# Attention scores of four tiles issued in one run, with the pooling matmuls and the values placed around them

## The chip, the core and the metric

The kernel runs on one core of a Trainium2 chip. The metric is device time in microseconds (us), the median of three runs of the whole program. The engines are named as the profile does: PE is TensorE's matmul pipe and PEld its weight loads, DVE is VectorE, ACT is ScalarE, POOL is GpSimd, SP is SyncE, which here only issues DMA transfers. Each engine works through its own instructions in order; engines wait for each other by semaphores.

## The reference, cut to what matters

The reference is one decoder block on x of 1024 positions by 1024 channels: a half-step feed-forward network, a mixer, a second half-step network, a final norm. The mixer projects the normed rows to q, k, v (12 heads of 64), to a pooling input and to two gates, and merges two branches:

```python
y_attn = dilated_mixture_attention(q, k, v) @ w_branch_attn[l]
y_pool = multiscale_pool(pz, pool_w[l], pool_scale[l]) @ w_branch_pool[l]
merged = gates[:, :, 0] * y_attn + gates[:, :, 1] * y_pool
h = h + merged @ w_out[l]
```

The attention has three groups of four heads, with windows and dilations (128, 1), (512, 4) and (2048, 16). In a group the positions with equal residue form a subsequence; each block of 128 queries of it sees its own block of keys and, where there is one, the block before, masked to a trailing window. Per query there are a maximum m of the scores, p = exp(s - m), its sum l, and the output p @ v / l. The three groups of a head slot are then weighted by their softmax denominators and added.

## The kernel before, in words

Everything is float32. A product is made of three matmuls on split operands (`three`: high x high, high x low, low x high), where high is a rounded copy and low the rest. Before the attention stage comes the projection of the mixer (line 332), behind it the branch product and merge (lines 1756 to 1776) and the second network. The change lies in the attention stage alone, between these two.

**Tiles and pairs.** The work is 48 tiles in order: head pair 0 with groups 0, 1, 2, then head pair 1 with groups 1, 2, 0, eight tiles of 128 queries in each. A tile treats two heads (a = 0, 1). It is *narrow* (one block of 128 keys) or *wide* (two blocks, 256 keys): group 0 has one narrow tile and seven wide ones, group 1 alternates, group 2 has narrow ones only. Two tiles form a pair q = 0 to 23, and the loop over q is a software pipeline written out by hand under a manual schedule: what is written first is issued first on its engine. Pairs 0 to 3 are group 0, 4 to 7 group 1, 8 to 11 group 2, 12 to 15 group 1, 16 to 19 group 2, 20 to 23 group 0.

**What is done for a pair**, each by a function with the name given:

- `scores` (L1553, tile `s`): per tile three terms for each of two heads, 12 matmuls of 64 rows, into two PSUM banks of the tag `mm`, one for each head.
- `masked` (L1571, tile `e`): on DVE, four custom operations, each adds mask and scale and takes the maximum of one head of one tile, with a short read of the accumulator (`stats`) behind each. Below these are called the maxima. They free the score banks.
- `exponents` (L1580): on ACT, four exponentials with their sums.
- `trans_p` (L1600, tile `tp`): 4, 6 or 8 transposes on PE into one or two banks of the tag `acc`.
- `split_p`: the high part on ACT (L1612, `ehi`) and the low part on DVE (L1615, `elo`); the low part frees the transposes' banks.
- `values` (L1633, tile `o`): 6, 9 or 12 matmuls into one bank of the tag `acc`.
- `gather` (L1651): four copies on DVE out of that bank into the rows of the group's output; below, the copies. They free the bank.

**Fills.** The pooling branch's product (`branch`, L1703, tile `yp`) is 16 chains of 12 matmuls. It is a generator, and each `next(fill)` issues four of them, called a fill; three fills end a chain, which holds one bank of the tag `acc`. `end_branches` then multiplies the chain's bank by a gate on DVE (L1717, tile `gb`: the gate product), which frees it. Every second chain ends a branch block: its rows are stored (L1726) and the weights and the gate of a later block are loaded (`load_branch`, L1241 and L1242).

**Banks.** `mm` and `acc` have four banks each. A new tile takes the bank that was released longest ago in program order, and its first writer waits on the semaphore of the last reader. From step 18 to 21 the tag `mm` is used by `factor_rows` too (L1534, tile `fa`: four transposes a time), whose banks are read by the products on DVE (L1670, tile `o`) of the first head pair's combination.

**One step q before.** PE: scores of q; transposes of q-1; two fills (one where q % 4 is 3); the factor rows, where there are any; values of q-2. DVE: copies of q-3; maxima of q; low part of q-1; products with the factor rows; gate products of the chains that ended. ACT: high part of q-1; parts of the next ring of q and k operands (L1213, with the low part on POOL, L1214); exponents of q. `house` and `load_ring` issue the small transfers: row statistics, values, the next ring (L1206). After the loop follow the transposes, values and copies that are left, the last fills and the combination of head pair 1. A reciprocal on DVE (L1514) in step 17 waits for sums on POOL (L1513).

Of the kernel before, what the change touches and what calls it, by code (L numbers as in the profile page):

```python
# [16 lines left out]
P = 128  # L17
# [8 lines left out]
HD = 64  # L26
SC = HD ** -0.5
GROUPS = 3
# [8 lines left out]
def tokens(g, i):  # L37

    if g == 0:
        return i * P, 1, (i - 1 if i > 0 else None)  # L40
    if g == 1:
        r, b = divmod(i, 2)
        return r + 4 * P * b, 4, (i - 1 if b else None)
    return i, 8, None
# [74 lines left out]
def three(hi_lo_l, hi_lo_r):  # L119

    lh, ll = hi_lo_l
    rh, rl = hi_lo_r
    return ((lh, rh), (lh, rl), (ll, rh))
# [3 lines left out]
def tile_block(  # L127
# [29 lines left out]
    ve, ac, gp, pe = nc.vector, nc.scalar, nc.gpsimd, nc.tensor  # L157
# [10 lines left out]
    def bank(tag, name):  # L168
        return psum.tile([P, HALF], F32, tag=tag, name=name)
# [1029 lines left out]
    ring = {}  # L1199
# [160 lines left out]
    with tc.manual_schedule():  # L1360
# [4 lines left out]
        for k in range(len(items) + 4):  # L1365
# [6 lines left out]
            if k < len(items):  # L1372
                q, m = items[k]
# [3 lines left out]
            if k - 1 in results:  # L1377
                q, m = items[k - 1]
# [40 lines left out]
    def open_w_o():  # L1419
        wo_pools.append(wo.enter_context(sbuf(f"wo{len(wo_pools)}", "right")))  # L1420
# [46 lines left out]
    slots = [(hp, g, i) for hp in range(HPAIRS) for g in ((0, 1, 2), (1, 2, 0))[hp] for i in range(NT)]  # L1467
    N = len(slots)
# [68 lines left out]
    def blocks(g, i):  # L1537

        return 1 if tokens(g, i)[2] is None else 2

    T = {}

    def scores(s):
        hp, g, i = slots[s]
        u = hp * GROUPS + g
        n = blocks(g, i)
        ks = slice((i + 1 - n) * P, (i + 1) * P)
        ps = [bank("mm", f"s{s}_{a}")[:, :n * P] for a in range(2)]
        (qhi, qlo, _), (khi, klo, _) = ring[u]
        for j, (l, r) in enumerate(three((qhi, qlo), (khi, klo))):  # L1550
            for a in range(2):
                rows = slice(a * HD, (a + 1) * HD)
                pe.matmul(ps[a], l[rows, i * P:(i + 1) * P], r[rows, ks], start=(j == 0), stop=(j == 2))  # L1553
        T[s] = {"s": ps}

    def masked(s):
        hp, g, i = slots[s]
        d = T[s]
        n = blocks(g, i)
        m0 = 0 if n == 2 else (128 if g < 2 else 256)  # L1560
        p = d.pop("s")
        if g == 0:
            st = stats[hp][:, 0, i, :]
        else:
            if i == 0:
                own_stats[hp, g] = att_small.tile([P, NT, 4], F32, name=f"own_stats{hp}_{g}")
            st = own_stats[hp, g][:, i, :]
        e = ep.tile([P, 4 * P], F32, tag="e", bufs=4, name=f"e{s}")
        e = e[:, :2 * n * P].rearrange("p (a c) -> p a c", a=2)
        for a in range(2):  # L1570
            ve.tensor_tensor_reduce(e[:, a, :], p[a], mask[:, m0:m0 + n * P], -SC, -NEG, OP.add, OP.min,  # L1571
                                    accum_out=st[:, a:a + 1])
        d.update(e=e, st=st)
# [11 lines left out]
    def pair(q):  # L1585

        ns = [2 * blocks(*slots[s][1:]) * P for s in (2 * q, 2 * q + 1)]
        return ((2 * q, 0, ns[0]), (2 * q + 1, ns[0], ns[1])), sum(ns)
# [16 lines left out]
    def split_p(q):  # L1605

        tiles, n = pair(q)
        hi = a2.tile([P, 2 * HALF], F32R, tag="ehi", name=f"ehi{q}")
        lo = a2.tile([P, 2 * HALF], F32R, tag="elo", name=f"elo{q}")
        todo = tp.pop(q)  # L1610
        for p, c0, w in todo:
            ac.activation(hi[:, c0:c0 + w], p, AF.Copy)  # L1612
        yield
        for p, c0, w in todo:
            ve.tensor_tensor(lo[:, c0:c0 + w], p, hi[:, c0:c0 + w].bitcast(F32), op=OP.subtract)  # L1615
        for s, c0, w in tiles:
            T[s]["pt"] = tuple(t[:, c0:c0 + w].rearrange("p (a b c) -> p a b c", a=2, c=P) for t in (hi, lo))
        yield

    def values(q):  # L1620
        both = bank("acc", f"o{q}")
        for s in (2 * q, 2 * q + 1):
            hp, g, i = slots[s]
            d = T[s]
            n = blocks(g, i)

            p = both[:, s % 2 * 2 * P:(s % 2 + 1) * 2 * P].rearrange("p (a c) -> p a c", a=2)
            pt = d.pop("pt")
            j, end = 0, 3 * n - 1
            for b in range(n):  # L1630
                c = slice((i + 1 - n + b) * P, (i + 2 - n + b) * P)
                for l, r in three(tuple(v[:, c] for v in v_of[hp * GROUPS + g]), tuple(w[:, :, b, :] for w in pt)):
                    pe.matmul(p, l, r, start=(j == 0), stop=(j == end))  # L1633
                    j += 1
            d["o"] = p
            if i == NT - 1:
                del v_of[hp * GROUPS + g]
# [3 lines left out]
    def gather(s):  # L1641

        hp, g, i = slots[s]
        p = T.pop(s)["o"]
        t0, step, _ = tokens(g, i)
        cols = slice(t0, t0 + step * (P - 1) + 1, step)
        if i == 0:
            own[hp, g] = sums_o.tile([P, S], F32, tag="o", bufs=HPAIRS * GROUPS, name=f"o{hp}_{g}")
        for a in range(2):
            r = slice(a * HD, (a + 1) * HD)  # L1650
            ve.tensor_copy(own[hp, g][r, cols], p[r, a, :])  # L1651
# [72 lines left out]
    def send():  # L1724
        while stores:
            nc.sync.dma_start(*stores.pop())  # L1726

    def branches():
        for n in range(2 * KT):
            yield from branch(n)  # L1730

    fill = branches()
# [45 lines left out]
    def advance(gen, n=1):  # L1778
        for _ in range(n):
            next(gen, None)  # L1780
# [24 lines left out]
    with tc.manual_schedule():  # L1805
        load_ring(uses[1], ring_tile)
        load_branch(1)
        factors = [make_factors(hp, eng) for hp, eng in enumerate((gp, ve))]
        combines = [[Combine(hp, half, adds, lower) for half in range(2)]
                    for hp, (adds, lower) in enumerate((((gp, gp), gp), ((gp, ve), ve)))]  # L1810
        splits = {}
        for q in range(N // 2):
            send()
            u, i = divmod(q, NT // 2)
            if 0 < u < len(uses) - 1 and i == 0:
                load_ring(uses[u + 1], ring_tile)
            scores(2 * q)
            scores(2 * q + 1)
            if q == 1:
                next(fill)  # L1820
                next(fill)
            if q > 0:
                trans_p(q - 1)
                splits[q - 1] = split_p(q - 1)
            if q > 1:
                next(fill, None)
                if q % 4 != 3:
                    next(fill, None)
            if q > 2:
                gather(2 * q - 6)  # L1830
                gather(2 * q - 5)
            masked(2 * q)
            masked(2 * q + 1)

            j = q - N // 4 - 6
            fa = [combines[0][j // 2]] * (2 - j % 2) if 0 <= j < 4 else []
            for f in fa:
                f.rows()
            if q > 1:
                values(q - 2)  # L1840
            if q > 0:
                advance(splits[q - 1], 2)
            for n in ((), (0,) if u > 0 else (), (2, 1) if u > 0 else (0, 2), (3,) if u > 0 else (1, 3))[i]:
                if u + 1 < len(uses):
                    split_ring(uses[u + 1], n)
            for f in fa:
                f.product()
            end_branches()
            exponents(2 * q)
            exponents(2 * q + 1)  # L1850
            house(2 * q)
            house(2 * q + 1)
        send()
        right_b.close()
        load_ya(3)
        load_merge(0)
        load_merge(1)
        open_w_o()
        q = N // 2
        trans_p(q - 1)  # L1860
        splits[q - 1] = split_p(q - 1)
        advance(factors[1])
        next(fill, None)
        values(q - 2)
        gather(2 * q - 6)
        gather(2 * q - 5)
        advance(splits[q - 1], 2)
        advance(factors[1], 2)
        next(fill, None)
        end_branches()  # L1870
        values(q - 1)
        for s in range(2 * q - 4, 2 * q):
            gather(s)
        for n in range(8):
            combines[1][n // 4].step()
            if n != 3:
                next(fill, None)
            end_branches()
            send()
            if n == 3:  # L1880
                load_merge(2)
        for k in (3, 4):
            load_merge(k)
# [34 lines left out]
    ops, banks = {}, {}  # L1918
# [66 lines left out]
    with tc.manual_schedule():  # L1985
# [66 lines left out]
        r = [rows_first2(t) for t in range(2)]  # L2052
# [211 lines left out]
```

## Time and profile before

| what | us |
|---|---|
| median of three runs (1908.35 to 1908.94) | 1908.75 |
| the profiled execution | 1909.05 |
| its span, first to last instruction | 1907.2 |
| PE busy / DVE busy / ACT busy / POOL busy | 1894.9 / 1337.5 / 760.0 / 731.2 |
| attention stage, first scores to first branch product | 1042.7 to 1159.8 |
| mean granted TensorE clock | 0.999 of full speed |

In the rows below, times are from the start of the span. "busy" is the union of the instructions of an engine in a stretch; PE's instructions are pipelined, so a busy PE can still start its matmuls late, and the distance between the starts of two matmuls tells more than their durations. DVE's rows overlap by up to 0.1 us at their ends as well, so its costs are taken from starts too. An idle time in brackets names what ended the wait.

### The profile page before, as it was taken

What the parts mean: (1) busy time and instruction counts of PE and PEld (TensorE: products, weight loads), DVE (VectorE), ACT (ScalarE), POOL (GpSimd) and SP (SyncE); (2) the same over time, 40 slices, a digit from 0 to 9 for tenths busy, and PEclk for the clock granted to TensorE, in tenths of its full rate; (3) what the DMA queues carried; (4) which work ended last, traced back from release to release, by engine and by line L of the source; (5) the groups of instructions that cost most, each with busy time, mean ns of one, the idle gap of its engine ahead of it and who ended that gap; (6) DMA issues with size and microseconds to landing.
All of it is one profiled execution on the core that took longest, in us unless ns stands there. A gap on an engine that the chain in (4) does not pass through costs nothing.

```text
span 1907.2 us, 24938 instructions
## 1 busy us (share of the span) xinstructions
PE 1894.9 (99%) x8946; PEld 1574.4 (83%) x8946; DVE 1337.5 (70%) x2017; ACT 760.0 (40%) x1364; POOL 731.2 (38%) x548
## 2 busy tenths in 40 slices
PE   9999999999999999999999999999999999999998
PEld 8888888888888888888888888888888888888886
DVE  7776556557776776667875896887665556577777
ACT  6323333333344443334444772353333323333344
POOL 5333333331233355444544456553333333312132
PEclk9999999999999999999999999999999999999999
DMA  4155222336466627655667977743433223454564
GB/s 189 50 193 177 83 88 105 138 110 215 148 233 219 204 92 248 220 213 196 229 231 288 305 231 262 269 149 121 164 120 124 84 88 116 149 194 138 194 219 166
DMA packets 144940, 331.98 MB, mean 174 GB/s; under 512 B 19120, under 2 KB 39856, under 8 KB 143280
## 3 DMA queue, kind: packets, MB, share of 16 engines
q1 hardware_dynamic: 137280, 308.00, 46.4%
q10 hardware_dynamic: 7536, 22.39, 3.3%
q8 instruction: 70, 1.15, 0.3%
q14 instruction: 54, 0.44, 0.1%
HBM read 229.61 MB, written 100.73 MB: 173 GB/s over the span
## 4 chain that ended last, share of the span: by engine, by line
PE 96%; DVE 1%; issue 1%; POOL 1%; ACT 1%; DMA 0%; SPq 0%; POOLq 0%; ACTq 0%; DVEq 0%
PE d_f L754 22%; PE u_mixm L332 18%; PE wo L1955 4%; PE yp L1703 2%; PE o L1633 1%; PE ya L1768 1%; PE s L1553 1%; PE u_f20b L332 1%; PE u_f11a L332 1%; PE u_f20a L332 1%; PE u_f11b L332 1%; PE u_f210b L332 1%; PE u_f210a L332 1%; PE u_f29b L332 1%; PE u_f29a L332 1%
## 5 line engine op out<-in xcount | busy, mean ns | idle before, releaser
L754 PE MATMUL d_f<-bhi_f,ahi_f 128*128 128x512 f32 x616 | 240.4, 390 | 0.0
L754 PE MATMUL d_f<-bhi_f,alo_f 128*128 128x512 f32 x616 | 239.8, 389 | 0.0
L754 PE MATMUL d_f<-blo_f,ahi_f 128*128 128x512 f32 x616 | 239.7, 389 | 0.0
L716 POOL TENSOR_TENSOR alo_f<-g_f,ahi_f 128x512 fp32r<-128x512 f32 x60 | 83.4, 1408 | 292.9 <-ACT ahi_f L712 285.7
L332 PE MATMUL u_mixm<-xhi_t_mix,wc_mixm 128*128 128x512 f32 x608 | 194.9, 391 | 0.1
L332 PE MATMUL u_mixm<-xhi_b_mix,wc_mixm 128*128 128x512 f32 x456 | 149.0, 392 | 0.0
L754 PEld LDWEIGHTS d_f<-bhi_f,alo_f 128*128 128x128 f32 x616 | 115.6, 188 | 24.2 <-DVE alo_f L716 0.3
L754 PEld LDWEIGHTS d_f<-bhi_f,ahi_f 128*128 128x128 f32 x616 | 115.6, 188 | 24.0 <-DVE xlo_b_mix L411 0.2
L754 PEld LDWEIGHTS d_f<-blo_f,ahi_f 128*128 128x128 f32 x616 | 115.6, 188 | 23.9
L332 PEld LDWEIGHTS u_mixm<-xhi_t_mix,wc_mixm 128*128 128x128 f32 x608 | 114.0, 188 | 24.3 <-POOL wc_mixm L309 0.8
L332 PE MATMUL u_mixm<-xlo_t_mix,wc_mixm 128*128 128x512 f32 x304 | 118.4, 389 | 0.0
L309 POOL TENSOR_TENSOR wc_mixm<-s_mixm,wc_mixm 128x512 fp32r<-128x512 f32 x52 | 73.5, 1415 | 101.7 <-ACT wc_mixm L304 90.6
L332 PEld LDWEIGHTS u_mixm<-xhi_b_mix,wc_mixm 128*128 128x128 f32 x456 | 85.6, 188 | 17.8 <-issue 0.3
L304 ACT ACTIVATE wc_mixm<-s_mixm 128x512 fp32r<-128x512 f32 x76 | 47.0, 628 | 117.3 <-DVE s_mixm L364 56.9
L332 PE MATMUL u_mixm<-xlo_b_mix,wc_mixm 128*128 128x512 f32 x228 | 88.8, 389 | 0.0
L712 ACT ACTIVATE ahi_f<-g_f 128x1024 fp32r<-128x1024 f32 x84 | 81.8, 974 | 2.3 <-DMA g_f<-gs_f 2.3
L309 POOL TENSOR_TENSOR wc_mixm<-raw,wc_mixm 128x512 fp32r<-128x512 f32 x40 | 61.0, 1530 | 44.1 <-ACT wc_mixm L304 37.2
L712 ACT ACTIVATE bhi_f<-s_f2w 128x512 fp32r<-128x512 f32 x55 | 32.7, 627 | 95.4 <-DVE s_f2w L732 87.8
L332 PEld LDWEIGHTS u_mixm<-xlo_t_mix,wc_mixm 128*128 128x128 f32 x304 | 57.1, 188 | 11.6
L712 ACT ACTIVATE bhi_f<-s_f1w 128x512 fp32r<-128x512 f32 x55 | 32.9, 629 | 84.0 <-DVE s_f1w L732 79.1
L716 DVE TENSOR_TENSOR alo_f<-g_f,ahi_f 128x1024 fp32r<-128x1024 f32 (+1 forms) x48 | 57.6, 1200 | 7.7 <-ACT ahi_f L712 7.7
L1955 PE MATMUL wo<-w_o,o_hi 128*128 128x512 f32 x224 | 60.2, 390 | 0.0
(1321 smaller groups left out, 5079.8 us busy)
## 6 DMA issues: line engine op xcount, KB each, us to landing
g_f<-gs_f SPq DMA_DIRECT2D x70, 512.0 KB
gs_f<-y_f SPq DMA_DIRECT2D x88, 256.0 KB
raw<-in_w2a_dram SPq DMA_DIRECT2D x35, 512.0 KB
raw<-in_w2b_dram SPq DMA_DIRECT2D x35, 512.0 KB
gs_f<-gb_f SPq DMA_DIRECT2D x46, 256.0 KB
raw<-in_w1a_dram SPq DMA_DIRECT2D x22, 512.0 KB
raw<-in_w3a_dram SPq DMA_DIRECT2D x22, 512.0 KB
raw<-in_w1b_dram SPq DMA_DIRECT2D x22, 512.0 KB
```

The lines of the kernel that those rows point to most:

```text
L304: ac.activation(w[:, 0], src, AF.Copy)
L309: eng.tensor_tensor(w[:, 1], src, w[:, 0].bitcast(F32), op=OP.subtract)
L332: pe.matmul(p, a, b, start=(start and i == 0), stop=(i == 11), skip_group_check=not start)
L712: ac.activation(hi[:, c], src, AF.Copy)
L716: eng.tensor_tensor(lo[:, d], src[:, o], hi[:, d].bitcast(F32), op=OP.subtract)
L754: pe.matmul(self.banks[m][t], l, r, start=(first and q == 0), stop=(last and q == 2))
L1553: pe.matmul(ps[a], l[rows, i * P:(i + 1) * P], r[rows, ks], start=(j == 0), stop=(j == 2))
L1633: pe.matmul(p, l, r, start=(j == 0), stop=(j == end))
L1703: pe.matmul(p, a, b, start=(j == 0), stop=(j == 11))
L1768: pe.matmul(p, a, b, start=(j == 0), stop=(j == 5))
L1955: pe.matmul(banks[m][t], l, r, start=(st == 0 and n == 0), stop=(st == 1 and n == 5))
```

## The change

Three things are moved; the arithmetic, the number of instructions and the transfers stay.

1. `scores` takes a pair, and both tiles of the pair share their two banks: tile 2q in the columns 0 to 255, tile 2q+1 in 256 to 511. Two pairs then fill the four `mm` banks, and a step with even q (a *long* step) issues the scores of q and of q+1 together. A step with odd q (a *short* step) issues none.
2. Values stand directly behind the transposes in a long step, ahead of its fills. A long step has two fills, a short one has one, and where q % 4 is 2 (but for q = 22) the long step has a third, which stands ahead of the factor rows and of the gate products.
3. In a long step DVE has the copies of q-3 ahead of the maxima of q, as before; in a short step the maxima come first. The factor rows stand behind the values in both.

```diff
-    def scores(s):
-        hp, g, i = slots[s]
...
-        ps = [bank("mm", f"s{s}_{a}")[:, :n * P] for a in range(2)]
+    def scores(q):
+
+        banks = [bank("mm", f"s{q}_{a}") for a in range(2)]
+        for s in (2 * q, 2 * q + 1):
+            hp, g, i = slots[s]
...
+            c0 = s % 2 * 2 * P
+            ps = [b[:, c0:c0 + n * P] for b in banks]
...
-            scores(2 * q)
-            scores(2 * q + 1)
+
+            even = q % 2 == 0
+            if even:
+                scores(q)
+                scores(q + 1)
             if q == 1:
                 next(fill)
                 next(fill)
             if q > 0:
                 trans_p(q - 1)
                 splits[q - 1] = split_p(q - 1)
+            if q > 1 and even:
+                values(q - 2)
             if q > 1:
                 next(fill, None)
-                if q % 4 != 3:
+                if even:
                     next(fill, None)
-            if q > 2:
+            if even and q > 2:
                 gather(2 * q - 6)
                 gather(2 * q - 5)
             masked(2 * q)
             masked(2 * q + 1)
+            if not even and q > 2:
+                gather(2 * q - 6)
+                gather(2 * q - 5)
 
             j = q - N // 4 - 6
             fa = [combines[0][j // 2]] * (2 - j % 2) if 0 <= j < 4 else []
-            for f in fa:
-                f.rows()
-            if q > 1:
+            if q > 1 and not even:
                 values(q - 2)
             if q > 0:
                 advance(splits[q - 1], 2)
+            if q % 4 == 2 and q < N // 2 - 2:
+                next(fill, None)
+            for f in fa:
+                f.rows()
```

The total of the fills up to the end of the loop is 40 in both; in steps 2 to 22 the new order is ahead by one fill at times (it has a third one in steps 2, 6, 10, 14 and 18, where the old order had two in every step but each fourth). The last lines of the step are as before: products with the factor rows, gate products, exponents, `house`.

More of the change, by code (lines that the diff above doesn't have):

```diff
@@ L1541, in tile_block @@
     T = {}
-    def scores(s):
-        hp, g, i = slots[s]
-        u = hp * GROUPS + g
-        n = blocks(g, i)
-        ks = slice((i + 1 - n) * P, (i + 1) * P)
-        ps = [bank("mm", f"s{s}_{a}")[:, :n * P] for a in range(2)]
[L1549 to L1554, printed above, removed]
+    def scores(q):
+        banks = [bank("mm", f"s{q}_{a}") for a in range(2)]
+        for s in (2 * q, 2 * q + 1):
+            hp, g, i = slots[s]
+            u = hp * GROUPS + g
+            n = blocks(g, i)
+            ks = slice((i + 1 - n) * P, (i + 1) * P)
+            c0 = s % 2 * 2 * P
+            ps = [b[:, c0:c0 + n * P] for b in banks]
+            (qhi, qlo, _), (khi, klo, _) = ring[u]
+            for j, (l, r) in enumerate(three((qhi, qlo), (khi, klo))):
+                for a in range(2):
+                    rows = slice(a * HD, (a + 1) * HD)
+                    pe.matmul(ps[a], l[rows, i * P:(i + 1) * P], r[rows, ks], start=(j == 0), stop=(j == 2))
+            T[s] = {"s": ps}
     def masked(s):
```

## The prediction

> **What bounds the kernel now.** I read the page first, then the granted clock and busy time by stretch, then the chain of work inside the attention stage, then single steps engine by engine.
>
> ```profile
> PE 1894.9 (99%) x8946; PEld 1574.4 (83%) x8946; DVE 1337.5 (70%) x2017; ACT 760.0 (40%) x1364; POOL 731.2 (38%) x548
> ...
> PE 96%; DVE 1%; issue 1%; POOL 1%; ACT 1%; DMA 0%; SPq 0%; POOLq 0%; ACTq 0%; DVEq 0%
> ```
>
> TensorE (PE) sets the end almost everywhere, so the change must be judged by how long PE takes for the attention stage, from 1042.4 us to the branch product at 1159.9 us. Nothing else is moved. The stage by stretches (columns: length, then busy time of PE, PEld, DVE, ACT, POOL, then clock, DMA share, GB/s):
>
> ```profile
> 1042.40:1054.20 11.80, 11.23 (x79) 8.30 (x77) 7.69 (x30) 10.05 (x29) 1.65 (x2) 1.00 1.03 395
> 1054.20:1077.50 23.30, 23.30 (x193) 20.62 (x192) 19.40 (x73) 17.63 (x59) 8.55 (x7) 1.00 0.87 302
> 1077.50:1118.90 41.40, 41.40 (x326) 35.87 (x322) 37.75 (x145) 31.48 (x111) 22.50 (x21) 1.00 0.87 270
> 1118.90:1146.40 27.50, 27.50 (x212) 23.91 (x211) 27.00 (x95) 18.46 (x63) 14.67 (x13) 1.00 0.72 222
> ```
>
> PE is full, but look at the third busy figure: VectorE (DVE) works 37.75 of 41.40 us and then 27.00 of 27.50 (98%). In steps 18 to 23 there are two bounds side by side. I write q for a step and its pair of tiles.
>
> **The gain.** Scores use 64-row matmuls; everything around them uses 128 rows. PE's rows around one set of scores:
>
> ```profile
> 1085.37 0.28 PE L1633 MATMUL o<-elo,v_in 128*128 128x256 f32 x1
> 1085.49 0.28 PE L1633 MATMUL o<-ehi,v_in 128*128 128x256 f32 x1
> 1085.70 0.33 PE L1553 MATMUL s<-qk_hi,qk_hi 64*128 64x128 f32 x2
> 1085.86 0.28 PE L1553 MATMUL s<-qk_in,qk_hi 64*128 64x128 f32 x2
> 1085.98 0.27 PE L1553 MATMUL s<-qk_hi,qk_in 64*128 64x128 f32 x2
> ...
> 1086.31 0.28 PE L1553 MATMUL s<-qk_hi,qk_in 64*128 64x128 f32 x2
> 1086.52 0.66 PE L1600 MATMUL tp<-ident,e 128*128 128x128 f32 x4
> ```
>
> Within values the next starts 0.12 later, into scores 0.21; the first scores take 0.16 instead of 0.12; out of them 0.21 instead of 0.11. That is 0.09 + 0.04 + 0.10 = 0.23, and the transposes behind scores lose a little more: eight take 1.02 there and 0.96 behind values (rows below). I take 0.3 us for one entry and exit. Steps 3, 5, ... 23 lose theirs: 11 x 0.3 = 3.3 us. At the start PE idles 11.80 - 11.23 = 0.57 us, mostly before the scores of step 1, which now find two untouched banks: another 0.6 (bounds 0 and 1.0). Largest gain 3.9 us.
>
> **What the steps become.** No matmul, copy or transfer is added. PE groups (start, time to the end of the group):
>
> ```profile
> 1118.16 0.82 PE s L1553 x12
> 1118.97 0.59 PE tp L1600 x4
> 1119.56 1.85 PE yp L1703 x8
> 1121.41 0.87 PE fa L1534 x8
> 1122.29 0.71 PE o L1633 x6
> ...
> 1131.62 1.17 PE s L1553 x12
> ...
> 1136.61 0.91 PE s L1553 x12
> ...
> 1142.36 1.02 PE tp L1600 x8
> ...
> 1144.31 1.44 PE o L1633 x12
> 1145.74 0.96 PE tp L1600 x8
> ```
>
> For narrow tiles a long step is now two scores 1.5 (0.82 + 0.82 less a switch), transposes 0.4, values 0.8, two fills 1.85 (three: 2.75): 4.5 or 5.5 us. A short step is transposes, one fill 0.95, values: 2.2 us. DVE's work stays the same in each step, and it stands in one queue. Its rows of steps 18, 7 and 21:
>
> ```profile
> 1118.75 0.25 DVE L1514 RECIPROCAL top<-top 128x16 f32<-128x16 f32 x1 [0.93 <-POOL top L1513]
> 1118.92 1.54 DVE L1651 COPY o<-o 64x128 f32<-64x128 f32 x4
> 1120.49 0.29 DVE L1571 CUSTOM_DVE_ANT_0 e<-s,mask 128x128 f32<-128x128 f32 x1
> ...
> 1121.34 0.69 DVE L1615 TENSOR_TENSOR elo<-tp,ehi 128x512 fp32r<-128x512 f32 x1
> 1121.94 1.28 DVE L1670 TENSOR_TENSOR o<-o,fa 128x512 f32<-128x512 f32 x2
> 1123.13 1.64 DVE L1651 COPY o<-o 64x128 f32<-64x128 f32 x4
> ```
>
> ```profile
> 1074.91 0.29 DVE L1571 CUSTOM_DVE_ANT_0 e<-s,mask 128x128 f32<-128x128 f32 x1
> ...
> 1076.03 1.02 DVE L1615 TENSOR_TENSOR elo<-tp,ehi 128x256 fp32r<-128x256 f32 x2
> 1076.96 0.68 DVE L1717 TENSOR_TENSOR gb<-yp,gb 128x512 f32<-128x512 f32 x1
> 1077.56 0.38 DVE L1651 COPY o<-o 64x128 f32<-64x128 f32 x1
> ```
>
> ```profile
> 1133.68 0.42 DVE L1571 CUSTOM_DVE_ANT_0 e<-s,mask 128x256 f32<-128x256 f32 x1
> ...
> 1135.07 1.02 DVE L1615 TENSOR_TENSOR elo<-tp,ehi 128x256 fp32r<-128x256 f32 x2
> ```
>
> By differences of starts: copies 1.6 (1.2 for undilated tiles, next fence), maxima 0.85 / 1.1 / 1.4 (four narrow, mixed, four wide), low part 0.6 / 0.95 / 1.2, product 0.6, gate product 0.6. So DVE needs 3 to 5 us in a short step in which PE has 2.2 to 3.4. It must have worked ahead in the long step, and there its queue stops: the gate product (and the products with fa) of a long step stand **before** the maxima of the short one and need PE's last work of the long step.
>
> PE in turn waits for DVE by the banks. In the built program values of steps 3, 5, 7, 13, 15, 21 and 23 go into the bank that the values of the step before left, and this is free only after its copies, which the short step now puts behind the maxima. Before, the copies stood first and the scores and fills covered them. That such a wait is paid in full is seen once, in the tail, where fills end early:
>
> ```profile
> 1146.38 1.19 DVE L1651 COPY o<-o 64x128 f32<-64x128 f32 x4
> ```
>
> ```profile
> 1147.00 0.63 PE L1703 MATMUL yp<-xhi_b_mix,wab 128*128 128x512 f32 x2
> 1147.71 0.36 PE L1633 MATMUL o<-ehi,v_in 128*128 128x256 f32 x1
> ```
>
> Copies end at 1147.57, values start at 1147.71: 0.1 us behind.
>
> **The walk.** Times from the start of the step named.
> Step 6 (mixed): scores 1.6, transposes 2.2, values 3.4, three fills 6.2. DVE: copies 1.2, maxima 2.4, low part 3.5, then the gate product of the branch that ends with the third fill: 6.2 to 6.85; maxima of step 7 to 8.0; copies to 9.6. PE in step 7: transposes to 6.75, fill (its bank waits for the gate product, 0.2) to 7.9, values only at 9.7. **Lost 2.0.**
> Step 12: DVE's copies end at 2.4 (it comes 0.75 late), maxima 3.5, low part 4.1, gate 4.7, maxima of 13 to 5.85, copies to 7.45. PE would have values at 6.3, gets them at 7.5: **lost 1.2.** Step 15 loses 0.2. Steps 9, 11 and 17 find their banks free. Up to step 18: start -0.6, eight switches -2.4, waits +3.4, some 0.1: step 18 starts 0.5 late.
> Step 18: PE scores 1.5, transposes 1.9, values 2.7, three fills 5.45, fa 6.3. DVE: the reciprocal waits for POOL as before, to 1.55, copies 3.15, maxima 4.0, low part 4.6, **idle to 6.0** for fa, two products 7.2, gate 7.8, maxima of 19 8.65, copies 10.3, low part 10.9, product 11.5. PE: transposes 6.7, fill 7.65, values (bank of the gate product) 8.75, fa 9.2; scores of 20 from 9.4; those of 21 need the bank of that last fa: 11.6 instead of 10.1, **lost 1.5**. The row of 1131.62 (1.17 against 0.91) is the same wait before, 0.26.
> Step 20: PE transposes 12.9, values 13.7, fills 15.55, fa 16.4. DVE copies 13.15, maxima 14.3, low part 14.9, idle to 16.0, products 17.2, gate 17.8, maxima of 21 19.2, copies 20.8. PE: transposes 17.0, fill waits for the gate to 17.9 (**0.9**), values for the copies, 18.8 to 20.9 (**2.1**), then 0.8 and fa 0.45: step 22 starts at 22.35. Before: 1136.61 - 1118.16 = 18.45. Lost 3.9 net.
> Step 22: fills end 27.9, gate 28.55, maxima 29.95, copies 31.15; values 31.25 instead of 29.75 (**1.5**), end 32.7. Before: 1145.74 - 1118.16 = 27.6. Lost 5.1 net.
> The tail has the same order, PE and DVE enter it equally late, so it hides nothing. Sum: 0.5 + 5.1 = **5.6 us later**. The profiled execution took 1909.05 (span 1907.2), 0.3 above the median 1908.75; from the median 1914.35.
>
> **Costs taken as nothing.** Activations keep their order; in a short step the transposes need exponents that have had the values and fills of the long step (2.6 us and more) as cover. SyncE's queue changes: the load of the third ring now stands behind a gate load and a store that wait for the end of branch 1.
>
> ```profile
> 1048.48 2.95 SPq L1206 DMA_DIRECT2D qk_in<-qk  x2
> ```
>
> At 395 GB/s each 0.52 MB takes 1.3 us; issued near 1059 with three in front it lands near 1064, and its first split stands behind the transposes of step 5, near 1065. If late, exponents queue behind it on ACT: 0 to 2 us.
>
> **Rivals.** (a) PE decides: if copies and gates never hold it, 1908.75 - 3.9 = 1904.9. For it: PE fills every stretch; against: the banks above. It decides if DVE's idle in long steps stays below about 0.5. (b) DVE decides and its order costs nothing: PE's gain is lost, idle DVE time is made up in the early stretch (19.40 of 23.30), so 1908.7. Against: from 1118.90 on there are 0.5 us to make up from. [...] (c) Worse: exponents or the ring's load late as well, 0.3 in each of 11 short steps: 1917.7.
>
> **How the numbers follow.** Forecast 0.55, (a) 0.10, (b) 0.22, (c) 0.13. The forecast's own range is 1912.0 to 1916.7: waits of 9.5 us (5.6 + 3.9), a quarter either way. About 0.2% (3.8 us) is what a measurement of this kernel tells from no change. Faster than that: half of (a), 0.05. Within: the rest of (a), (b) and a tenth of the forecast, 0.33. Slower: 0.62. The range 1906.0 to 1918.5 leaves out half of (a), the upper part of (c) and the forecast's ends.
>
> **What would show it.** Right: PE (or its weight loads) waiting for DVE's copies in the odd steps, 6 to 9 us in all, the largest in steps 7, 13, 21 and 23; DVE idle before gate products and products with fa; twelve score groups of 24 matmuls with one 0.2 us entry each; the stretch of steps 18 to 23 lengthened by 5. Wrong: copies that end before PE's short-step fill does, or values that start behind the fill without a gap; then DVE ran ahead and (a) or (b) holds.

## The result, and the profile after

The changed kernel takes 1916.92 us (median of six runs, 1914.16 to 1921.01) against 1908.85 us for the kernel before (six runs, 1908.35 to 1909.92): 1.0045 times as long, 95% interval 1.0035 to 1.0056. The forecast was 1914.4 with a range of 1906.0 to 1918.5. In the changed kernel the lines of the functions stand 4 lower: scores L1557, maxima L1575, transposes L1604, values L1637, copies L1655, product with fa L1674, fills L1707, gate product L1721.

The profiled execution took 1920.11 (span 1917.7). Its page, busy time and the chain:

```profile
PE 1898.2 (99%) x8946; PEld 1579.5 (82%) x8946; DVE 1338.6 (70%) x2017; ACT 760.0 (40%) x1364; POOL 730.1 (38%) x548
...
PE 94%; DVE 2%; issue 1%; POOL 1%; ACT 1%; DMA 0%; SPq 0%; POOLq 0%; ACTq 0%; DVEq 0%
```

The whole page hardly differs from before: PE still has 99%, and only its share of the chain fell from 96% to 94%. The stretches that the prediction used show more (length, busy PE, PEld, DVE, ACT, POOL, then granted clock, DMA share, GB/s):

```profile
1042.40:1054.20 11.80, 11.59 (x92) 9.31 (x91) 8.75 (x37) 10.69 (x32) 2.55 (x2) 1.00 1.04 389
1054.20:1077.50 23.30, 21.67 (x167) 19.07 (x165) 18.28 (x67) 17.18 (x56) 7.63 (x6) 0.97 0.84 300
1077.50:1118.90 41.40, 40.12 (x306) 35.07 (x305) 35.51 (x140) 28.42 (x99) 18.57 (x16) 0.93 0.80 242
1118.90:1146.40 27.50, 23.38 (x174) 19.98 (x174) 21.52 (x69) 14.69 (x52) 17.04 (x18) 0.90 0.66 203
```

PE was full in the last three of these before; now, in the same stretches of time, it lacks 1.63, 1.28 and 4.12 us, and, what the prediction has nothing of, the granted clock is below 1. What PE waited for in the stage, and what DVE waited for (us in total, times, longest):

```profile
PE o L1637 <- DVE o L1655: 5.7, 4, 1.8
PE s L1557 <- DVE o L1674: 1.3, 1, 1.3
PE yp L1707 <- DVE gb L1721: 0.9, 1, 0.9
PE o L1637 <- DVE gb L1721: 0.2, 1, 0.2
```

```profile
DVE gb L1721 <- PE yp L1707: 7.5, 6, 2.5
...
DVE o L1674 <- PE fa L1534: 3.5, 3, 1.6
```

The first group is the forecast wait: values for copies, four times (steps 7, 13, 21 and 23). The second is the other half of the circle: DVE idles for PE's last fill and last fa of a long step, and then PE waits until DVE has caught up. The chain through step 21 (start, length, what) shows it in one row after another:

```profile
1136.73 0.45 PE fa L1534 x4
1137.17 0.02 issue
1137.20 1.29 DVE o L1674 x2
1138.48 0.60 DVE gb L1721
...
1140.12 0.34 DVE e L1575
...
1141.56 0.40 DVE o L1655
1141.96 0.14 issue
1142.10 1.62 PE o L1637 x6
```

fa, two products, gate product, four maxima, four copies, and only then PE's values. For 4.9 us (1137.20 to 1142.10) the chain lies on DVE alone.

The clock's part, by stretches cut where it changes:

```profile
1076.27:1083.10 6.83, 6.83 (x45) 6.49 (x44) 3.83 (x15) 1.44 (x5) 0.00 (x0) 0.50 1.13 329
...
1141.13:1147.95 6.82, 5.85 (x37) 5.33 (x38) 5.09 (x17) 1.10 (x3) 1.77 (x2) 0.50 0.96 273
```

Twice TensorE runs at half clock for 6.83 us, each time right behind or in one of the stalls (steps 7 and 21). The six runs of the kernel fall in three groups: 1914.16 at a mean clock of 0.999; 1916.16, 1916.75 and 1917.10 at 0.997 to 0.998; 1920.11 and 1921.01 at 0.995. Only the trace of 1920.11 is kept, with its two stretches; by their mean clock the other groups fit none and one. If so, the first stretch costs 2.6 us (the middle of the second group less the first) and two cost 6.4, about 3 us each, and without any the loss is 1914.16 - 1908.85 = 5.3 us, which rests on a single run.

### The profile page after: what moved, and what is told of

Its sections match the earlier page's. It is cut to its first block, busy times and chain, and to the rows that moved or that the text cites. A ratio compares the mean times of both kernels' runs of the same rounds, so it can differ in the third digit from the quotient of the medians.

```text
span 1917.7 us, 24947 instructions
## 1 busy us (share of the span) xinstructions
PE 1898.2 (99%) x8946; PEld 1579.5 (82%) x8946; DVE 1338.6 (70%) x2017; ACT 760.0 (40%) x1364; POOL 730.1 (38%) x548
## 4 chain that ended last, share of the span: by engine, by line
PE 94%; DVE 2%; issue 1%; POOL 1%; ACT 1%; DMA 0%; SPq 0%; POOLq 0%; ACTq 0%; DVEq 0%
PE d_f L754 22%; PE u_mixm L332 18%; PE wo L1969 4%; PE yp L1707 2%; PE o L1637 1%; PE ya L1772 1%; PE u_f11a L332 1%; PE u_f20b L332 1%; PE u_f20a L332 1%; PE u_f11b L332 1%; PE u_f26a L332 1%; PE u_f15a L332 1%; PE u_f210b L332 1%; PE u_f210a L332 1%; PE u_f29b L332 1%
```

## The experiments

**Theory 1**: PE loses by waiting for DVE in the short steps, because the long step's products and gate products and then the maxima stand in DVE's one queue ahead of the copies; the stalls also bring the half clock. **Rivals**: grouping the scores is itself the loss; DVE's load decides in whatever order; the half clock has nothing to do with the stalls. The edits are shortened to what matters. Each run stands against the kernel before on the same chip; its medians were 1909.21 (the first four), 1908.66 (the next four), 1908.93 (the three after these) and 1909.00 (the last).

**Copies first again in the short steps.** The other parts of the change stay.

```
-            if even and q > 2:
+            if q > 2:
                 gather(2 * q - 6); gather(2 * q - 5)
             masked(2 * q); masked(2 * q + 1)
-            if not even and q > 2:
-                gather(2 * q - 6); gather(2 * q - 5)
```

> The changed kernel, but in the short steps the copies stand ahead of the maxima again, as before the change. Theory 1 (PE waits for DVE because the copies stand behind the maxima and the gate product in one queue; after such a stall the granted clock halves for 6.83 us): the waits of values for copies, 1.2 to 1.8 us each in steps 7, 13, 21 and 23, shrink by the 0.85 to 1.4 us of the maxima, 4.5 to 5 us in all, some of it paid again as a wait of the long steps' transposes for late exponents; no stretch at clock 0.5; 1908 to 1911. Rival (grouping the scores itself costs the time, or DVE's load does whatever its order): 1914 or more.

Measured: 1912.32 (10 runs), 3.11 above before, ratio 1.0018 (1.0008 to 1.0027); clock 0.999. PE's waits:

```profile
PE s L1557 <- DVE o L1674: 0.9, 2, 0.5
PE yp L1707 <- DVE gb L1721: 0.9, 1, 0.9
PE o L1637 <- DVE o L1655: 0.8, 2, 0.5
PE s L1557 <- DVE own_stats L1575: 0.6, 1, 0.6
PE tp L1604 <- ACT e L1584: 0.4, 1, 0.4
```

The wait for copies falls by 4.9 us (5.7 to 0.8), as theory 1 said, and the half clock is gone from the profiled run. But 1.0 us comes back behind maxima and exponents, which are now late, and the time lies 1.3 above the expected 1911: the rest of the change, with fills, values and fa in their new order, loses 3 us even with copies first. DVE has the same work as in the changed kernel here, so the order alone gave back 8.07 - 3.11 = 5.0 us, the half clock included; this refutes that DVE's load decides in whatever order.

**The third fill moved to the short step.**

```
-            if q % 4 == 2 and q < N // 2 - 2:
-                next(fill, None)
...
-                if even:
+                if even or (q % 4 == 3 and q < N // 2 - 1):
                     next(fill, None)
```

> The changed kernel, but the third fill of the steps 2, 6, 10, 14 and 18 stands in the short step behind it, behind that step's own fill and ahead of its values. Theory 1: the gate product no longer stands ahead of the short step's maxima there and PE has 0.95 us more of its own to do; the wait of step 7 (1.5 us) and the first stretch at half clock go, those of steps 21 and 23 stay, and step 21 may still halve the clock: 1909 to 1913. Rival (the place of the fills does nothing, DVE's load decides): 1914 to 1920.

Measured: 1913.96 (7 runs), 4.75 above before. Step 7's wait and its half clock are gone, but the total of the waits for copies is hardly smaller, since step 19 has a new one:

```profile
PE o L1637 <- DVE o L1655: 5.2, 4, 1.8
```

The time lies 1.0 above the upper end of what theory 1 gave and just under the rival's 1914: both ranges are missed, and the run tells little between them, except that step 21's wait stays and the clock behind it is halved for one 3.41 us stretch, in the profiled run.

**PE kept busy in the waits.**

```
+        for _ in range({4: 6, 12: 7, 13: 5}.get(n, 0)):
+            pe.matmul(p, *todo[0], start=True, stop=True)
```

> The changed kernel, with 6, 7 and 5 more matmuls of 128x512 at the start of the fills of steps 7, 21 and 23: each repeats the fill's first product, which the next one overwrites, so that PE works where it otherwise waits for the copies. That adds 18 x 0.23 = 4.1 us of work in waits of 1.5, 1.76 and 1.2 us. Theory 1: the work lies in the waits, no stretch falls to half clock, and the time is that of the changed kernel without such a stretch: 1913.5 to 1915 in every run, with a spread under 1 us, and faster than the changed kernel's median although PE does more. Rival (the half clock has another cause): the clock stays at 0.995 to 0.998 of full in the span and the time at 1916 to 1921.

Measured: 1915.48 (five runs, 1914.05 to 1916.84), 6.27 above before. The profiled run has no half clock anywhere in the stage:

```profile
1042.40:1160.00 117.60, 112.96 (x867) 97.23 (x866) 100.22 (x363) 80.84 (x264) 47.51 (x43) 1.00 0.80 258
```

PE does 4 us more, and the median lies 1.4 us under the changed kernel's, but the runs of the two overlap, so that the gain is not clear of noise. That the clock stays up in the profiled run speaks for the stalls as the cause of the half clock; but two of the five runs (1916.81 and 1916.84) still have a clock of 0.998, so "in every run" was wrong, and the median lies above the expected 1915. The waits in steps 13 and 20 were not filled. The spread, 2.8 us, is less than the changed kernel's 6.9.

**The scores grouped, and nothing else.** The loop of before, but for this:

```
-            scores(2 * q); scores(2 * q + 1)
+            if q % 2 == 0:
+                scores(q); scores(q + 1)
```

Here scores(q) writes both tiles of a pair, as in the change.

> The kernel before, with only the scores of two pairs set together in the even steps: fills two, two, two, one, copies ahead of the maxima, values behind the fills, rows of fa ahead of values, all as before. Theory 1 (grouping gains 0.3 us for each of 11 switches and 0.6 at the start, and the order of the rest makes the losses): 1905 to 1909, no wait over 1 us for copies and no half clock. Rival (an even step's long run of scores and a short step's lack of them starve DVE and PE by turns in any order): 1912 or more.

Measured: 1908.14 (10 runs), 1.07 below before, ratio 0.9995 (0.9986 to 1.0004); clock 0.999. Grouping is no loss. How much it gains is read from the starts of the scores in steps 0, 20 and 22, first of the kernel before, then of this one:

```profile
1042.67 0.33 PE L1553 MATMUL s<-qk_hi,qk_hi 64*128 64x128 f32 x2
...
1126.52 0.33 PE L1553 MATMUL s<-qk_hi,qk_hi 64*128 64x128 f32 x2
...
1136.54 0.39 PE L1553 MATMUL s<-qk_hi,qk_hi 64*128 64x256 f32 x2
```

```profile
1041.97 0.33 PE L1557 MATMUL s<-qk_hi,qk_hi 64*128 64x128 f32 x2
...
1123.85 0.32 PE L1557 MATMUL s<-qk_hi,qk_hi 64*128 64x128 f32 x1
...
1134.88 0.39 PE L1557 MATMUL s<-qk_hi,qk_hi 64*128 64x256 f32 x2
```

From the first scores to step 20: 83.85 before, 81.88 now, a gain of 1.97; to step 22: 93.87 and 92.91, a gain of 0.96. (The expectation of the next run but one speaks of 2.67 and 1.66: these still hold 0.70 by which the whole stage began earlier.) The forecast term was 3.9, of which 3.3 by step 20 (0.6 and nine switches). The starts of PE's groups between the scores of step 2 and those of step 20 show where the rest went. Scores and values together take 2.6 us less (15.80 + 20.00 before, 13.83 + 19.35 now), 0.29 for each of nine switches, so the price of an entry and exit was read rightly. Transposes take 0.8 more (11.29 and 12.07) and fills 0.3 more, and up to step 2 the gain was 0.4, not 0.6. What the transposes lose fits a wait that the grouping adds, their weight loads for exponents; of before and of this kernel:

```profile
PEld tp L1600 <- ACT e L1580: 1.3, 4, 0.5
```

```profile
PEld tp L1604 <- ACT e L1584: 3.1, 11, 0.4
```

**Half of the short steps' copies on ACT.** 
```
+            if a == 1 and s // 2 % 2 == 0 and s // 2 + 3 < N // 2:
+                ac.activation(own[hp, g][r, cols], p[r, a, :], AF.Copy)
+            else:
                 ve.tensor_copy(own[hp, g][r, cols], p[r, a, :])
```

> The changed kernel, its order untouched, but in the short steps one of the two copies of each tile is made by ACT, so DVE's queue there is two copies (0.75 us) shorter. Theory 1 (values wait in the short steps for the copies at the end of DVE's queue, and the half clock comes from these waits): the four waits of 1.2 to 1.8 us become 0.4 to 1.1 us, no stretch at half clock, 1909.5 to 1912. Rival (the place of the copies in the queue is not what holds PE, or ACT becomes the late one): 1914 or more.

Measured: 1923.93 (four runs), 15.27 above before: far outside theory 1's range, and in the rival's, which allowed for ACT becoming the late one. The first row is what ACT waited for, then the copies of step 7:

```profile
ACT o L1656 <- DVE o L1658: 25.3, 21, 3.6
```

```profile
1074.41 0.37 DVE L1658 COPY o<-o 64x128 f32<-64x128 f32 x1
1074.88 0.39 ACT L1656 ACTIVATE o<-o 64x128 f32<-64x128 f32 x1 [2.62 <-DVE o L1658]
1075.30 0.37 DVE L1658 COPY o<-o 64x128 f32<-64x128 f32 x1 [0.52 <-ACT o L1656]
1075.71 0.39 ACT L1656 ACTIVATE o<-o 64x128 f32<-64x128 f32 x1 [0.44 <-DVE o L1658]
```

All four copies of a step read one bank and write one buffer, and they run one behind another although ACT's and DVE's touch different rows; whether the bank or the buffer orders them is not shown. So nothing was shortened, 0.41 to 0.47 us from start to start, and ACT stood waiting for 25.3 us in all with its high parts and exponents queued behind. The run tests a different thing than it was made for; what it shows is the price of such a hand-over.

**The same split in steps 18 to 23 alone**, in the kernel with the scores grouped, and in the kernel before: the same edit under another condition.

```
+            if a == 1 and 18 <= s // 2 + 3 < N // 2:
```

> The kernel before with the scores alone grouped (as in e4_scores_only, 1908.14), and in steps 18 to 23 one of the two copies of each tile made by ACT. Theory 1 (with the scores grouped PE was 2.67 us ahead of the kernel before at step 20 and 1.66 at step 22, because DVE, 98% full there, became the bound): DVE has 0.75 us less in each of six steps, the lead stays near 2.7 us to the end, 1906.4 to 1907.3. Rival (the lead is lost to something else): 1908 to 1909.

> The kernel before, with the same copies on ACT in steps 18 to 23 and nothing else changed. Theory 1 (before, PE alone set the end there, DVE was full but never waited for): no change, 1908.7 to 1909.5. Rival (the relief of DVE is a gain of its own, and the grouping adds nothing to it): 1907 to 1908.

Measured: 1908.99 (11 runs), 0.33 above before, and 1910.13 (11 runs), 1.47 above before. The first lies at the end of its rival's range, the second above both of its own. The hand-over just described is in both: DVE's copies wait 6.0 us for ACT's in either kernel, and ACT's 4.9 and 4.5 us for DVE's. So the runs don't tell what holds the lead; the difference between the two, 1.14, is again about the gain of grouping alone.

**Maxima first, and the scores grouped, with fills, values and fa as before.** On the kernel with the scores grouped:

```
-            if q > 2:
+            if even and q > 2:
                 gather(2 * q - 6); gather(2 * q - 5)
             masked(2 * q); masked(2 * q + 1)
+            if not even and q > 2:
+                gather(2 * q - 6); gather(2 * q - 5)
```

> The kernel before with the scores grouped (e4_scores_only, 1908.14) and, besides, the maxima ahead of the copies in the short steps; fills two, two, two, one and values behind them as before. Theory 1 (maxima first cost PE a wait where a short step has little work of its own and a gate product ahead of it): the short steps 7, 11, 15, 19 and 23 with one fill wait up to 1.2 us each, those with two fills little; 1909 to 1913. Rival (the order of DVE costs nothing by itself): 1907.5 to 1908.7.

Measured: 1909.24 (10 runs), 0.58 above before, clock 0.999, at the lower end of theory 1's range. PE's waits for copies stand in steps 13 and 23:

```profile
PE o L1637 <- DVE o L1655: 1.1, 2, 0.7
```

A longer one, 1.6 us, stands in step 21, which has two fills, where the theory expected little. The profile names nothing that ended it, but PE's fill goes on 0.1 us behind the end of DVE's copies (1132.65 + 1.58 = 1134.23), so a bank that these free is the likely reason:

```profile
1132.65 1.58 DVE L1655 COPY o<-o 64x128 f32<-64x128 f32 x4
```

```profile
1134.33 0.93 PE L1707 MATMUL yp<-xhi_b_mix,wab 128*128 128x512 f32 x3 [1.56 <-issue]
```

So maxima first costs 0.58 + 1.07 = 1.65 us by itself. The new order of fills, values and fa costs 3.11 + 1.07 = 4.18 with copies first. If the two simply add, they would be 5.8; the change has 8.07 + 1.07 = 9.1, and the 3.3 beyond is about what the half clock takes, which neither part brings on alone (a clock of 0.998 in one of the ten runs with copies first, 0.999 in all ten here).

**Waits made on purpose.** In the kernel with the scores grouped, DVE makes 4, 10 and 17 copies of a small tile ahead of three fills, and one extra matmul needs the last of them.

```
+        for _ in range({2: 4, 4: 10, 7: 17}.get(n, 0)):
+            ve.tensor_copy(held, ones)
+        if n in (2, 4, 7):
+            pe.matmul(p[:, :P], held, ones, start=True, stop=True)
```

> The kernel before with the scores alone grouped (e4_scores_only, 1908.14, no half clock), in which PE is made to wait three times: ahead of the fills that begin branches 2, 4 and 7 (steps 4, 7 and 12) DVE makes 4, 10 and 17 copies of 128x128, the last of which a small extra matmul needs. Waits of about 0.7, 2 and 3.4 us, 15 to 20 us apart. Theory 1 (the clock halves for 6.83 us behind a 3.41 us window in which PE was busy for about half or less, so single gaps of under 2 us can do it): the first wait gives no half clock, the last one does, the middle one can; 1908 plus the waits plus 2.6 us for each half clock, 1914 to 1920. [...]

Measured: 1919.35 (four runs), within theory 1's range. Only the second and the third wait came about, 1.6 and 4.7 us. PE's busy time (the first number behind the length) in a stretch of 3.41 us around the first and in one that ends in the second, and the stretch behind the latter:

```profile
1078.52:1081.93 3.41, 1.84 (x10) 1.46 (x9) 3.13 (x14) 0.72 (x2) 0.00 (x0) 1.00 0.99 310
1099.01:1102.42 3.41, 0.68 (x7) 0.44 (x5) 3.10 (x11) 1.50 (x3) 1.26 (x1) 1.00 1.06 404
1102.42:1109.24 6.82, 4.83 (x14) 4.06 (x15) 5.30 (x22) 1.87 (x8) 0.00 (x0) 0.50 0.57 181
```

Behind the single wait of 1.6 us, with PE busy for 0.54 of the 3.41 us, the clock stays whole; in the long one, after 3.41 us with 0.20, it is halved for 6.82 us. From the scores of step 12 to those of step 14 PE takes 15.34 us here (1094.25 to 1109.59) and 7.91 with the scores alone grouped (1090.63 to 1098.54), 7.4 more, of which the wait is 4.7; so the half-clock stretch costs about 2.7. Since the long wait exceeds 3.41 us by itself, the run alone doesn't show whether waits of under 2 us can do it, as theory 1 has it; the last section sets the stretches of all runs together.

**All four copies on ACT in steps 7, 13, 21 and 23**, the changed kernel's order untouched.

```
+            if s // 2 + 3 in (7, 13, 21, 23):
+                ac.activation(own[hp, g][r, cols], p[r, a, :], AF.Copy)
+            else:
                 ve.tensor_copy(own[hp, g][r, cols], p[r, a, :])
```

> The changed kernel with its order untouched, but all four copies of the short steps 7, 13, 21 and 23 made by ACT, so that no copy of ACT waits for one of DVE in the same step. Theory 1 (these copies at the end of DVE's queue hold PE): the four waits of values for copies, 5.7 us, fall under 2 us in all, no half clock, 1908.5 to 1912. Rival (DVE's or ACT's load holds PE whatever copies): 1914 or more.

Measured: 1908.50 (10 runs), 0.43 below before, ratio 0.9999 (0.9990 to 1.0008), clock 0.999. Sixteen copies taken out of DVE's queue give back the whole 8 us. PE's waits:

```profile
PE s L1557 <- DVE o L1677: 1.5, 2, 1.3
PE yp L1710 <- ACT o L1656: 0.9, 3, 0.5
PE o L1637 <- DVE gb L1724: 0.2, 1, 0.2
```

No wait for copies is left in front of values; 0.9 us of waiting for copies, now ACT's, stands ahead of fills. The run takes the copies off DVE's load as well as out of its queue, so by itself it doesn't part the two; copies first, with DVE's work unchanged, did. Together the two runs settle the main cause.

**The same for steps 19, 21 and 23, with the scores alone grouped.**

```
+            if s // 2 + 3 in (19, 21, 23):
```

> The kernel before with the scores alone grouped (e4_scores_only, 1908.14), and all four copies of the steps 19, 21 and 23 made by ACT. Theory 1 (DVE's full queue in steps 18 to 23 takes back 1 to 1.3 us of the 2.7 that grouping gains; the copies split between ACT and DVE in e6 only made the two wait for each other): the lead of 2.7 us at step 20 stays, 1906 to 1907.3. Rival (copies on ACT delay its exponents, and the transposes wait for these): 1908 to 1910.

Measured: 1906.95 (11 runs, 1906.10 to 1907.55), 1.98 below before, ratio 0.9988 (0.9980 to 0.9997). It beats both kernels and lies within theory 1's range. PE waits for DVE or ACT only 0.4 us in the stage:

```profile
PE yp L1710 <- ACT o L1656: 0.2, 1, 0.2
PE s L1557 <- DVE o L1677: 0.2, 1, 0.2
```

**fa at its old place**, on top of the run with sixteen copies on ACT.

```
+            for f in fa:
+                f.rows()
             if q > 1 and not even:
                 values(q - 2)
             if q > 0:
                 advance(splits[q - 1], 2)
             if q % 4 == 2 and q < N // 2 - 2:
                 next(fill, None)
-            for f in fa:
-                f.rows()
```

> The kernel of e10_short_copies_act (1908.5, no half clock), with the rows of fa back ahead of the values of a short step and ahead of the third fill of a long one. Theory 1 (with fa late, DVE's products with it come late, and the second scores of step 20 and of 22 wait for their bank, 1.3 and 0.2 us): these waits shrink by at least 1 us in all, 1906.7 to 1907.7. Rival (DVE, full in steps 18 to 23, has the products late whenever fa comes, or fa waits for its own bank instead): 1908 to 1909.

Measured: 1907.92 (11 runs), 1.08 below before, between the two ranges. The wait of the scores for the product fell only from 1.5 to 1.2 us, and the time by 0.6 against before, about the spread of these runs. The rival is the better description: DVE no longer idles for fa in step 18, yet the product of step 19, which frees the bank, comes only 0.4 us sooner after the start of step 18, for DVE has no gap up to it from the reciprocal of step 18 on. That reciprocal itself waits 2.1 us for POOL (0.9 before the change); what those sums cost was not tested.

## Why the prediction was right, step by step

**The bound** was read rightly: PE decides, DVE has next to no room from step 18 on, and the loss is PE waiting for DVE. All waits stand in the steps named, and the walk through step 18 fits: 9.36 us from its scores to those of step 20 (1120.89 to 1130.25), 9.4 forecast.

**The waits.** Forecast 9.5 us (5.6 + 3.9), measured 5.7 + 1.3 + 0.9 + 0.2 = 8.1. Values for copies in steps 7, 13, 21 and 23: 2.0 + 1.2 + 2.1 + 1.5 = 6.8 forecast, 1.5 + 1.1 + 1.8 + 1.4 measured, 5.7 in all. The gate product ahead of step 21's fill: 0.9 and 0.9. The second scores of step 20: 1.5 and 1.3; that their bank is the cause is right, that fa's place makes it late mostly not (the last experiment). The reciprocal of step 18 waits longer than "as before" (2.1 us, not 0.9), but the wait for fa behind it covered that.

**The gain** is the mis-sized term: 3.9 forecast (0.6 and 11 x 0.3), about 3 in the changed kernel's order. This follows from the run with sixteen copies on ACT, which still has 2.6 us of waits on PE and is 0.43 faster than before. The entry and exit of 64-row scores cost what the rows said, 0.29 a switch; which rows lose the rest in this order was not found. With the scores alone grouped the gain was less, 1.97 by step 20 and 0.96 by step 22: there the weight loads wait 3.1 us for exponents instead of 1.3, which the prediction took as covered (in the changed kernel it is covered: 1.4), and DVE, full from step 18, takes back 1 us. The last is the mechanism of rival (b): in those steps DVE, which empties the banks, is busy for 27.02 of 27.50 us (1118.90 to 1146.40), and copies moved to ACT brought about 1 us (1906.95 against 1908.14). They did so where a step's copies went to ACT whole (1906.95), and not where the two engines shared a tile (1908.99 and 1923.93).

**The sum.** 8.1 of waits against a gain of about 3 is 5.1; the run without half clock lost 5.3, the forecast was 5.6. Two errors, 1.4 in the waits and about 1 in the gain, cancel; that the forecast sum was nearer than its terms is luck.

**What was left out**: the clock. The prediction charged an idle PE its idle time alone. In five of six runs, by their mean clock, one or two of the stalls also halved it, for 6.83 us each in the kept trace. One such stretch, 2.6 us, is the difference between the forecast 1914.4 and the median 1916.92, which lies just above the forecast's own range of 1912.0 to 1916.7; the wider range held it only because of the room left for the rivals. That stalls bring it is shown in one direction by the runs that take them away (1912.32 and 1908.50: a clock of 0.999 in 19 of 20 runs) and in the other by the made wait of 4.7 us. The waits kept filled fit it in the profiled run and in three of five runs.

**The rivals.** (a), no wait at all, was refuted in the changed kernel, and its 1904.9 was not reached even where PE hardly waited (1906.95), since the forecast gain is twice what grouping brought in the best run (1.98). (b), DVE decides and its order costs nothing, was refuted by copies first: the order alone was worth 5.0 us. (c), late exponents or a late third ring, did not happen in the changed kernel: PE's waits list neither, and its weight loads waited 1.4 us for exponents, 1.3 before. Its 1917.7 is nearer to the median than the forecast is, but by the half clock and not by its own mechanism.

## What to carry to other kernels

When work is put together on one engine, ask what the engine that empties its results has at the head of its queue at that moment: a product that needs the last of the long run blocks everything behind it, and the buffers that the short run needs come free last. The cheapest cure here was not the order but the queue: sixteen small copies moved to an engine with room, whole steps of them, gave back 8 us. And a stall on TensorE is to be charged with the slow clock that may follow it: in the changed kernel 6.83 us at half clock, by the medians about 2.6 us more, behind stalls that left PE busy for 0.51 and 0.52 of the 3.41 us before.

## What the runs showed of the hardware

**Half clock in or behind stalls.** In the attention stage the half clock lasted 6.83 us at a time in the changed kernel and 3.41 us with the fill moved (1139.14 to 1142.55). In both traces that have two such stretches these begin a whole number of times 3.41 us apart: in the changed kernel 1141.13 - 1076.27 = 64.86 us, 19 times 3.414, and in the run with half of the short steps' copies on ACT 1144.13 - 1089.52 = 54.61 us, 16 times 3.413. The 3.41 us ahead of the two drops of the changed kernel, and three stretches as long, a whole number of times 3.41 us away, with stalls that brought none (PE busy is the first number behind the length):

```profile
1072.86:1076.27 3.41, 1.78 (x9) 1.11 (x8) 3.34 (x15) 3.02 (x11) 1.27 (x1) 1.00 0.68 222
1100.17:1103.58 3.41, 2.23 (x14) 1.53 (x13) 3.34 (x15) 2.85 (x11) 1.18 (x1) 1.00 1.04 392
1130.89:1134.30 3.41, 2.11 (x25) 1.77 (x22) 3.31 (x8) 0.28 (x1) 2.10 (x2) 1.00 0.03 5
1137.71:1141.12 3.41, 1.74 (x9) 0.98 (x7) 3.40 (x13) 2.58 (x9) 1.28 (x1) 1.00 0.38 136
...
1151.37:1154.78 3.41, 2.24 (x14) 1.49 (x12) 3.06 (x13) 2.65 (x10) 0.00 (x0) 1.00 0.20 71
```

Busy for 0.52 and 0.51 of the stretch: halved. For 0.65, 0.62 and 0.66: not. With the made waits 0.20 halved, 0.54 did not; with the fill moved 0.45 halved. No single wait of PE in the changed kernel is over 1.8 us. Drops of different traces, each counted from its own span's start, do not lie so: 1089.52 - 1076.27 = 13.25 us is 3.88 times 3.41. Whether that has to do with the spread of one kernel's times is not shown, with one trace of each kernel. PE's busy share alone does not tell the cases apart: in the run with half of the short steps' copies on ACT, one stretch led to the half clock with a busy share of 0.70 (the half clock follows from 1089.52 to 1092.93), and one of 0.53 did not:

```profile
1086.11:1089.52 3.41, 2.40 (x21) 1.69 (x20) 2.94 (x12) 2.99 (x12) 2.44 (x2) 1.00 0.89 252
...
1133.89:1137.30 3.41, 1.81 (x19) 1.68 (x20) 3.08 (x9) 2.31 (x11) 2.52 (x2) 1.00 0.03 5
```

What exactly sets the half clock off stays open. So does why it lasts 3.41 us in some cases and 6.83 in others.
